# Norm's roots and their spreading taken apart, and six operands made one product earlier, in a hybrid retention block

## The chip, the core and the metric

The kernel runs on one core of one Trainium2 chip. Its engines work side by side, each through a queue of its own: TensorE (PE; its weight loads are listed as PEld), VectorE (DVE), ScalarE (ACT), GpSimd (POOL, nearly unused here) and SyncE (SP), which issues most of the transfers. The metric is the device time of one execution in microseconds, as the median of several runs.

## What is computed

One layer on 1024 tokens of 1024 channels, in float32: `h = x + 0.5 SwiGLU_1(RMSNorm(x))`, then a mixing layer, then a second SwiGLU, then a last RMSNorm. Cut to what the change touches:

```python
h = h + 0.5 * swiglu_ffn(rmsnorm(h, norm_ffn1), ffn1_w_in, ffn1_w_out)
u = rmsnorm(h, norm_mix)
proj = u @ w_in                     # q, k, v, gates and pooled part
```

Here `rmsnorm(x, g) = x * rsqrt(mean(x*x) + eps) * g`, the mean being over the channels of a token, and `swiglu_ffn(x) = (silu(x @ gate) * (x @ up)) @ w_out`. The change lies where the first SwiGLU's last product ends and the projection of the mixing layer begins.

## The kernel before

**Precision.** Each float32 operand is split in two: a high half by ScalarE (lines 157 to 163, a cast) and the rest, the low half, by VectorE. A product takes three matmuls, high by high, high by low and low by high (`mm3`, lines 176 to 180). So each operand of 128 x 512 costs one cast on ScalarE and one operation on VectorE, and each weight tile the same. `operand` (line 165) makes such a pair in a buffer of the tag mv (28 of them); `weights` (line 170) makes one in a buffer of the tag wt (5).

**Seven products.** The large products are done in Strassen's manner, on blocks of half the size. In the groups of the projection (`strassen`, named t0, t1, p0, ... after what they project) the seven products are L11 by R11, S2 by T2, S1 by T1, S3 by T3 (body `b7`, line 492, which asks for the bank `e`), L12 by R21 (`b2`, line 499, which adds to the bank `a` of the first), S4 by R22 and L22 by T4 (`b4`). L and S are blocks of the weights and their combinations, R and T blocks of the normalised input and theirs. The first two groups, t0 and t1, are taken together, product by product, in this order.

**The input of the projection.** The object `mix` of the class `Next` gathers it: the rows of the first SwiGLU's result, multiplied by the channel gains, are split into R11, R22, R21, T1 to T4. The division by the root of each token is not done on the operands but on the results of the products (`mix.rms()`, a tile of 128 x 1024 named n2rb). For it, squares are added up in the tile n2ssq as results appear (`square`, line 255). `stats` (line 398) then does two things. `roots` adds over the channels with small matmuls (`token_sums`, line 224, into the bank n2sum, line 228) and takes the inverse root of 8 numbers per partition (`inverse_root`, line 206: lines 214 to 221, a root on ScalarE and five small operations on VectorE). `rows` spreads the result over the partitions, in two halves (`spread`, line 232). For each half, the numbers are split in two in the single buffer r2, ScalarE (line 245) and VectorE (line 243) each scale four 128 x 128 identity squares by them, and two matmuls with a matrix of ones add these up in a bank (n20b and n21b, line 246), which ScalarE copies out (line 406).

**The first SwiGLU's second half** is `ffn_out` (line 813). It makes its seven products P1, P6, P2, P7, P5, P3 and P4, each in 11 steps over the inner dimension. A step has a `prep`, which loads and splits weights and operand, and a `body` with its 12 matmuls. P3 multiplies by blocks R22 and P4 by blocks T4, both read from DRAM by `both` (line 840), which loads two steps' blocks into one buffer of the tag tl (4 of them). The names in the trace are bp3w and bp3m, bp4w and bp4m for weights and operands of these products, and bp6b for P4's four banks. After P4's last step, `after4` (line 987) adds the last rows and calls `end(4)`.

**What sets the order.** `Flow.run` (line 65) calls each step's `prep` four steps ahead of its `body`, and after each `body` takes two pieces of work from a queue, `flow.back`. `end_of` (line 1095) fills that queue at the end of P2, P5, P3 and P4; after P4 it adds R21 and T4 (four pieces each, lines 331 and 337), and then `roots` and `rows`. So the program has R21, T4, roots and spread between the bodies of the first products of t0 and t1, and the spread just ahead of S3 by T3 of t0. This program order is a preference: when the program is built, each engine's queue is filled by Tile with what is ready first, the earlier in the program having precedence. Buffers and banks of one tag go round.

Of the kernel before, what the change touches and what calls it, by code (L numbers as in the profile page):

```python
# [21 lines left out]
H = S // 2  # L22
DFF = 2816
FT = DFF // P
FH = FT // 2
# [65 lines left out]
def block_kernel(ctx: ExitStack, tc, x, x_tok, vecs, f1_in, f1_out, w_in, w_v, pool_w, w_ret, w_pool, w_o,  # L91
# [16 lines left out]
    def mv(name):  # L108
        return sb.tile([P, 2, H], F32R, tag="mv", bufs=N_MV, name=name)
# [26 lines left out]
    def load(dst, src):  # L136
        nc.sync.dma_start(dst, src)
# [8 lines left out]
    def half(t, j):  # L146
        return t[:, j * H : (j + 1) * H]
# [9 lines left out]
    def split(hi, lo, src):  # L157
        copy(hi, src)  # L158
        tt(lo, src, hi.bitcast(F32), SUB)  # L159
# [5 lines left out]
    def operand(src, name):  # L165
        m = mv(name)
        split(m[:, 0], m[:, 1], src)
        return m

    def weights(src, name, at=0):  # L170
        w = wt(name, at)
        n = src.shape[-1] // P
        split(flat(w, 0, n), flat(w, 1, n), src)
        return w

    def mm3(dst, w, m, start, stop):

        mm(dst, w[0], m[0], start=start, stop=False, skip_group_check=True)  # L178
        mm(dst, w[0], m[1], start=False, stop=False, skip_group_check=True)  # L179
        mm(dst, w[1], m[0], start=False, stop=stop, skip_group_check=True)  # L180

    def parts(m, at=slice(None)):
        return m[:, 0, at], m[:, 1, at]
# [629 lines left out]
    def ffn_out(nx, ops, ready, w, res, name, sink, end, last=None):  # L813
# [3 lines left out]
        R, T, B, T4 = ops  # L817
# [22 lines left out]
        def both(key, k, src):  # L840

            if k % 2 == 0:
                t[key] = (tl if key[0] != "L" else raw)(f"{name}{key}{k}")
                n = min(2, FH - k)
                for z in range(n):
                    load(half(t[key], z), src(k + z))
            return half(t[key], k % 2)
# [53 lines left out]
        def p3(k):  # L901
            return half(S2[k // 2], k % 2), both("R22", k, lambda z: T[z][:, H:])

        def p4(k):
            return both("L22", k, lambda z: w[z, :, 2 * H : 3 * H]), both("T4", k, lambda z: T4[z])

        bk = {}

        def step(n, f, k, where, start, after):
            o = {}  # L910

            def prep():
                L, X = f(k)
                o["w"] = weights(L, f"{name}{n}w{k}")
                o["m"] = operand(X, f"{name}{n}m{k}")

            def body():
                if start and k == 0:
                    for i in range(4):
                        bk[where, i] = (sum_bank if where == "b" and i < N_SUM else bank)(f"{name}{n}{where}{i}")  # L920
                for i in range(4):
                    mm3(bk[where, i], parts(o["w"], i), parts(o["m"]), start and k == 0, k == FH - 1)
                    if k == FH - 1:
                        after(i)

            return prep, body
# [75 lines left out]
        if not last:  # L1002
            for k in range(FH):
                yield step("p4", p4, k, "b", False, after4)
            return

        L, X = {}, {}
# [4 lines left out]
        def near(k):  # L1012
            def prep():
                l, r = p4(k)
                scale(r, r, 0)
                L[k], X[k] = operand(l, f"{name}p4w{k}"), mv(f"{name}p4m{k}")
                split(X[k][:, 0], X[k][:, 1], r)

            def body():
                if k == 1:  # L1020

                    last.seed(2, bk["a", 0])
                    last.seed(3, bk["a", 1])
                for n in range(2):
                    turned(n, k)
                    if k == FH - 1:
                        last.finish(n)

            return prep, body
# [56 lines left out]
    def ffn1():  # L1086
        for n, step in enumerate(ffn_in(first, f1_in, ops1, "a", lead)):
            flow.rate = 1
            yield step
        flow.rate = 2  # L1090
        yield from ffn_out(first, ops1, ops_done["a"], f1_out, x, "b", mix.quarter, end1)
# [2 lines left out]

    def end_of(nx):
        def end(part):
            nx.work(*{2: (nx.r11,), 5: (nx.r22, nx.p22), 3: (nx.t2, nx.t1, nx.t3), 4: (nx.r21, nx.t4_)}[part])
            if part == 4:
                nx.stats()

        return end

# [529 lines left out]
    def after(nx):  # L1632

        def t2(i):
            nx.r22(i)
            nx.t2(i)

        return {0: nx.r11, 4: nx.r21, 1: t2, 3: nx.t3, 2: nx.t1, 6: nx.t4_, 5: nx.p22}
# [179 lines left out]
    def second():  # L1818
        for n, step in enumerate(ffn_in(ffn2, f2_in, ops2, "c")):
            flow.rate = 1  # L1820
            yield step
        flow.rate = 2
    flow.run(chain(ffn1(), projections(), retention(), merge(), second(),
                   ffn_out(ffn2, ops2, ops_done.setdefault("c", set()), f2_out, h2, "d", fin.quarter, fin.end, fin)))
    flow.some(-1)

# [85 lines left out]
```

## Time and profile before

| | us |
|---|---|
| median of 3 runs | 2161.24 |
| lowest and highest | 2161.03, 2163.37 |
| profiled execution | 2160.41 |
| its span, first to last instruction | 2158.6 |
| mean granted TensorE clock | 0.998 |

The profile is of one execution. Times in it count from the start of the span. A row of the timeline has the start, the time from it to the end of the last instruction of the group, the engine, the line, the operation, what is written and read, the count, and in brackets the idle time of the engine ahead of it with what ended it. Durations of neighbouring instructions overlap by some hundredths on VectorE and ScalarE, and by nearly half on TensorE.

In that execution P3 runs from 573.5 to 603.4, P4 from 603.5 to 633.4, and the first products of t0 and t1 follow.

### The profile page before, as it was taken

The numbers are of one execution on the slowest core, as the hardware profiler recorded it, in microseconds if no ns is written. First come the engines' busy times: TensorE is split into PE (matmuls) and PEld (weight loads), VectorE is DVE, ScalarE is ACT, GpSimd is POOL, SyncE is SP. The second block draws the span as 40 slices with busy tenths as digits, with TensorE's granted clock in tenths as the row PEclk, the third lists the DMA queues.
The fourth block names the chain that finished last, engine by engine and source line by source line (L and its number), as shares of the span: only waits on it lengthen the run. The fifth ranks groups of instructions, "written<-read, shape, count | busy, mean of one in ns | idle before, by whom it ended". The sixth has DMA issues, their size and how long they took to land.

```text
span 2158.6 us, 29681 instructions
## 1 busy us (share of the span) xinstructions
PE 2143.2 (99%) x10668; PEld 1813.2 (84%) x10668; DVE 1849.4 (86%) x3247; ACT 1089.6 (50%) x2049; POOL 0.2 (0%) x4
## 2 busy tenths in 40 slices
PE   9999999999999999999999999999999999999998
PEld 7888888888887888888888898887888888888887
DVE  8788888997988798899767877899988878899796
ACT  8544454453655444444426754446644544445454
POOL 0000000000000000000000000000000000000000
PEclk9999999999999999999999999999999999999999
DMA  7232423585522333333485567624123232358642
GB/s 256 84 123 74 138 83 127 181 290 178 183 95 102 114 127 108 107 118 109 156 273 185 167 222 256 229 93 161 69 89 132 74 128 92 127 180 290 198 131 99
DMA packets 120131, 320.91 MB, mean 149 GB/s; under 512 B 13232, under 2 KB 17456, under 8 KB 119984
## 3 DMA queue, kind: packets, MB, share of 16 engines
q1 hardware_dynamic: 119408, 317.98, 43.4%
q8 instruction: 83, 1.36, 0.3%
q10 hardware_dynamic: 576, 1.05, 0.1%
q14 instruction: 64, 0.52, 0.1%
HBM read 228.27 MB, written 90.70 MB: 148 GB/s over the span
## 4 chain that ended last, share of the span: by engine, by line
PE 92%; DVE 5%; ACT 1%; issue 1%; DMA 1%; SPq 0%; ACTq 0%; DVEq 0%
PE c_b L178 2%; PE c_b L180 2%; PE c_b L179 2%; PE a_b L178 2%; PE a_b L179 2%; PE a_b L180 2%; PE c_e L178 2%; PE a_e L179 2%; PE c_e L179 2%; PE a_e L178 2%; PE c_e L180 2%; PE a_e L180 2%; PE a_a L179 1%; PE a_a L180 1%; PE a_a L178 1%; PE c_a L179 1%
## 5 line engine op out<-in xcount | busy, mean ns | idle before, releaser
L179 PE MATMUL c_b<-n3T,c_wS 128*128 128x512 f32 x176 | 68.5, 389 | 0.0
L180 PE MATMUL c_b<-n3T,c_wS 128*128 128x512 f32 x176 | 68.5, 389 | 0.0
L178 PE MATMUL c_b<-n3T,c_wS 128*128 128x512 f32 x176 | 68.2, 389 | 0.0
L178 PE MATMUL a_b<-n1T,a_wS 128*128 128x512 f32 x168 | 65.4, 389 | 0.0
L179 PE MATMUL a_b<-n1T,a_wS 128*128 128x512 f32 x168 | 65.4, 389 | 0.0
L180 PE MATMUL a_b<-n1T,a_wS 128*128 128x512 f32 x168 | 65.3, 389 | 0.0
L178 PE MATMUL a_a<-n1R,a_wL 128*128 128x512 f32 x120 | 46.7, 389 | 0.0
L180 PE MATMUL a_a<-n1R,a_wL 128*128 128x512 f32 x120 | 46.7, 389 | 0.0
L179 PE MATMUL a_a<-n1R,a_wL 128*128 128x512 f32 x120 | 46.7, 389 | 0.0
L179 PE MATMUL c_a<-n3R,c_wL 128*128 128x512 f32 x112 | 43.7, 390 | 0.0
L180 PE MATMUL c_a<-n3R,c_wL 128*128 128x512 f32 x112 | 43.6, 389 | 0.0
L178 PE MATMUL c_a<-n3R,c_wL 128*128 128x512 f32 x112 | 43.6, 389 | 0.0
L180 PEld LDWEIGHTS c_b<-n3T,c_wS 128*128 128x128 f32 x176 | 33.0, 188 | 6.9
L178 PEld LDWEIGHTS c_b<-n3T,c_wS 128*128 128x128 f32 x176 | 33.0, 188 | 6.9
L179 PEld LDWEIGHTS c_b<-n3T,c_wS 128*128 128x128 f32 x176 | 33.0, 188 | 6.8
L159 DVE TENSOR_TENSOR a_wS<-a_S,a_wS 128x512 fp32r<-128x512 f32 x45 | 30.6, 682 | 9.2 <-ACT a_wS L158 9.1
L178 PEld LDWEIGHTS a_b<-n1T,a_wS 128*128 128x128 f32 x168 | 31.5, 188 | 6.6
L180 PEld LDWEIGHTS a_b<-n1T,a_wS 128*128 128x128 f32 x168 | 31.5, 188 | 6.6
L179 PEld LDWEIGHTS a_b<-n1T,a_wS 128*128 128x128 f32 x168 | 31.5, 188 | 6.5
L159 DVE TENSOR_TENSOR c_wS<-c_S,c_wS 128x512 fp32r<-128x512 f32 x46 | 31.3, 681 | 3.7 <-ACT c_wS L158 3.7
L178 PE MATMUL c_e<-n3T,c_wS 128*128 128x512 f32 x88 | 34.4, 391 | 0.0
L179 PE MATMUL c_e<-n3T,c_wL 128*128 128x512 f32 x88 | 34.4, 391 | 0.0
(3067 smaller groups left out, 8053.8 us busy)
## 6 DMA issues: line engine op xcount, KB each, us to landing
c_ra<-in_f_in SPq DMA_DIRECT2D x22, 512.0 KB, 3.6
c_rb<-in_f_in SPq DMA_DIRECT2D x22, 512.0 KB, 4.3
a_ra<-in_f_in SPq DMA_DIRECT2D x21, 512.0 KB, 3.5
a_rb<-in_f_in SPq DMA_DIRECT2D x21, 512.0 KB, 4.2
t<-au SPq DMA_DIRECT2D x11, 512.0 KB, 4.2
b<-ag SPq DMA_DIRECT2D x11, 512.0 KB, 3.6
r<-au SPq DMA_DIRECT2D x11, 512.0 KB, 3.7
br<-r SPq DMA_DIRECT2D x11, 512.0 KB, 5.5
```

Of the source, the lines that this page charges most:

```text
L159: tt(lo, src, hi.bitcast(F32), SUB)
L178: mm(dst, w[0], m[0], start=start, stop=False, skip_group_check=True)
L179: mm(dst, w[0], m[1], start=False, stop=False, skip_group_check=True)
L180: mm(dst, w[1], m[0], start=False, stop=stop, skip_group_check=True)
```

## The change

Two edits. In `end_of`, the end of P4 no longer queues R21 and T4 ahead of `stats`; it hands them to `stats` as the work between its two parts, so that the queue holds `roots`, R21 and T4 (eight pieces), `rows`. In `ffn_out`, the preps of P3's steps 5 to 10 also load T4's blocks 0 to 5 and make their operands; P4's first six preps take these over. The second SwiGLU, which passes `last`, is left as it was.

```diff
+        def t4s(k):
+            return both("T4", k, lambda z: T4[z])
+
+        ahead = {}
+
         def p4(k):
-            return both("L22", k, lambda z: w[z, :, 2 * H : 3 * H]), both("T4", k, lambda z: T4[z])
+            return both("L22", k, lambda z: w[z, :, 2 * H : 3 * H]), ahead.pop(k) if k in ahead else t4s(k)
...
                 L, X = f(k)
                 o["w"] = weights(L, f"{name}{n}w{k}")
-                o["m"] = operand(X, f"{name}{n}m{k}")
+                o["m"] = X if len(X.shape) == 3 else operand(X, f"{name}{n}m{k}")
+                if n == "p3" and not last and k >= FH // 2:
+                    z = k - FH // 2
+                    ahead[z] = operand(t4s(z), f"{name}p4m{z}")
...
     def end_of(nx):
         def end(part):
-            nx.work(*{2: (nx.r11,), 5: (nx.r22, nx.p22), 3: (nx.t2, nx.t1, nx.t3), 4: (nx.r21, nx.t4_)}[part])
             if part == 4:
-                nx.stats()
+                nx.stats(between=[lambda f=f, i=i: f(i) for f in (nx.r21, nx.t4_) for i in range(4)])
+            else:
+                nx.work(*{2: (nx.r11,), 5: (nx.r22, nx.p22), 3: (nx.t2, nx.t1, nx.t3)}[part])
```

## The prediction

> **What bounds the kernel now.** I read the page first, then TensorE's waits, then the windows around the longest of them, then the timeline there. The page says that TensorE is the bound. The waits show how little of it is idle, and that the two longest waits are at line 246, the two matmuls that spread the roots of mix.
>
> ```profile
> PE 2143.2 (99%) x10668; PEld 1813.2 (84%) x10668; DVE 1849.4 (86%) x3247; ACT 1089.6 (50%) x2049; POOL 0.2 (0%) x4
> PE n20b L246 <- ACT n20dg L245: 2.3, 1, 2.3
> PE n21b L246 <- ACT n21dg L245: 1.6, 1, 1.6
> PE t0b L178 <- ACT t0v L479: 0.9, 1, 0.9
> ```
>
> The windows show a second cost behind the waits. The columns are the stretch, its length, then busy time with the count for PE, PEld, DVE, ACT and POOL, the granted clock, the DMA share and GB/s. The clock is at half from 662 to beyond 668, and only there.
>
> ```profile
> 650.00:655.00 5.00, 5.00 (x31) 4.34 (x30) 5.00 (x9) 3.29 (x6) 0.00 (x0) 1.00 0.01 3
> 655.00:660.00 5.00, 3.57 (x16) 2.63 (x14) 4.93 (x14) 4.52 (x9) 0.00 (x0) 1.00 0.27 88
> 662.00:664.00 2.00, 0.55 (x1) 0.50 (x2) 0.71 (x4) 1.40 (x5) 0.00 (x0) 0.50 0.55 203
> 666.00:668.00 2.00, 2.00 (x6) 1.52 (x6) 0.00 (x0) 0.00 (x0) 0.00 (x0) 0.50 0.00 0
> ```
>
> The timeline of TensorE gives the loss. A matmul in the undisturbed stream starts 0.227 us after the one before it (its duration of 0.39 overlaps the next).
>
> ```profile
> 658.18 0.39 PE L180 MATMUL t1a<-n2R,t1wL 128*128 128x512 f32 x1
> 660.86 1.02 PE L246 MATMUL n20b<-n20dg,ones_r 128*128 128x512 f32 x2 [2.29 <-ACT n20dg L245]
> 663.45 1.22 PE L246 MATMUL n21b<-n21dg,ones_r 128*128 128x512 f32 x2 [1.57 <-ACT n21dg L245]
> 664.47 0.63 PE L178 MATMUL t0e<-n2T,t0wS 128*128 128x512 f32 x1
> 668.74 0.41 PE L179 MATMUL t0e<-n2T,t0wS 128*128 128x512 f32 x1
> ```
>
> The last product of L12 and R21 lets the next matmul in at 658.41. The next product, S3 by T3 (t0e), starts at 664.47, and its first ten matmuls take 4.27 us where the full pace takes 2.27. So it stands as if it had begun at 666.47 at full pace. From 658.41 that is 8.06 us, of which four spreading matmuls need 0.9. **About 7.15 us are lost here**, and that is nearly all there is to win at this place.
>
> Why does TensorE stand still? VectorE has no free moment before the spread. After the last sum of squares it works on without a gap; the sums on TensorE were ready long before VectorE took them up.
>
> ```profile
> 645.40 0.68 DVE L265 TENSOR_TENSOR n2ssq<-n2ssq,n2q 128x512 f32<-128x512 f32 x1
> 646.00 1.40 DVE L163 SCALAR_TENSOR_TENSOR n2R<-bacc,vec,n2R 128x512 fp32r<-128x512 f32 x2
> 647.33 0.68 DVE L159 TENSOR_TENSOR t0wS<-t0rb,t0wS 128x512 fp32r<-128x512 f32 x1
> 647.93 1.41 DVE L163 SCALAR_TENSOR_TENSOR n2R<-bacc,vec,n2R 128x512 fp32r<-128x512 f32 x2
> 651.12 1.84 PE L228 MATMUL n2sum<-cst,n2ssq 128*128 128x1 f32 x16
> 655.51 1.28 DVE L159 TENSOR_TENSOR n2T<-bacc,n2T 128x512 fp32r<-128x512 f32 x2
> 656.72 0.15 DVE L214 TENSOR_SCALAR n2v<-n2sum 128x8 f32<-128x8 f32 x1
> 656.80 0.68 DVE L454 TENSOR_TENSOR t0S<-t0ra,t0S 128x512 f32<-128x512 f32 x1
> 658.00 0.19 DVE L216 RECIPROCAL n2r<-n2r 128x8 f32<-128x8 f32 x1
> 658.22 0.17 DVE L218 TENSOR_TENSOR n2t<-n2r,n2v 128x8 f32<-128x8 f32 x1
> 658.42 0.17 DVE L219 SCALAR_TENSOR_TENSOR n2t<-n2t,n2r 128x8 f32<-128x8 f32 x1
> 659.11 0.16 DVE L221 SCALAR_TENSOR_TENSOR n2r<-n2t,n2r 128x8 f32<-128x8 f32 x1
> 659.86 0.68 DVE L159 TENSOR_TENSOR t0wL<-t0rb,t0wL 128x512 fp32r<-128x512 f32 x1
> 660.47 0.86 DVE L243 TENSOR_SCALAR n20dg<-cst,n20r 128x128 fp32r<-128x128 f32 x4
> ```
>
> Note one more thing: t0e had its weights from 648.0 on (t0wS, third row), and still stands behind both spreads. Its bank is asked for behind theirs in the program, and the banks of one tag seem to be handed out in that order. So L12 by R21, whose banks are open, is all that can cover the spread, before and after.
>
> **The change, part by part.** *The roots move.* In the program they now follow the four last additions, ahead of R21 and T4; the spread follows T4 as before. The sums need n2ssq, complete at 646.08. TensorE is then in the product S1 by T1, and the 16 small matmuls fall into it: the same 1.84 us, only earlier, so TensorE reaches L12 by R21 at 652.8 as now. I take 0 for it; 0.6 us is the upper end, if TensorE's queue holds the sums ahead of that product, which began at 645.52. VectorE gets n2v at about 648.6, behind three of the R21 operations. Its five small operations cost 0.15 + 0.19 + 0.17 + 0.17 + 0.16 = 0.84 us, and the root is there at about 650.5, nine microseconds earlier than at 659.27.
>
> *What that delays.* The 0.84 us are not new, but they now lie ahead of T4 and of the weights of L12. The low half of those weights is what L12 by R21 waits for:
>
> ```profile
> 652.99 0.68 DVE L159 TENSOR_TENSOR t0wL<-t0ra,t0wL 128x512 fp32r<-128x512 f32 x1
> 653.85 0.40 PE L180 MATMUL t0a<-n2R,t0wL 128*128 128x512 f32 x1
> ```
>
> Four matmuls with the high half run from 652.8 to 653.7, and then TensorE waits. With 0.84 us more on VectorE, and some rounding of its order, the wait grows by **0.9 us** (ends: 0, if the order puts these weights first; 1.5, if a combination of weights slips in as well).
>
> *What that brings.* T4's last operation (the row at 655.51) now ends 0.9 later, at about 657.6, and the spread follows at once. The root's wait is gone, and so is the work that ran ahead of the spread: from 656.80 to 660.47 VectorE made two combinations S4 and three low halves of weights. These five, 3.0 us, stand behind the spread in the program and can follow it, since their products come after t0e and t1e. ScalarE scales its four squares earlier, in its own gaps. VectorE's four take 0.86, so the first half of the spread is complete at about 658.6. The second half uses the one buffer r2 again, so it cannot start earlier; from the end of VectorE's first four (661.33) to n21b (663.45) it took 2.12 us. So n21b starts at 660.7, and t0e 0.5 us after it, at **661.25**.
>
> *What TensorE does until then.* L12 by R21 ends at 658.41 + 0.9 = 659.3, and the two matmuls of n20b, taken in between, make it 659.8. It waits **0.9 us** for n21b. So the gain is 666.47 - 661.25 = **5.2 us**, which is the 7.15 lost now less two waits of about 0.9 each and rounding.
>
> *The clock.* That sum leaves out the half clock. In the trace the pause of 0.9 at t0b (645.5) left it at full, and 2.29 + 1.57 us with two matmuls between them halved it for some 6 us. Two pauses of 0.9, six microseconds apart, lie by the first; if the clock fell after them as it does now, the ten slow matmuls' 2.0 us would come back and make 2158.1. The Trainium skill ("TensorE: Matmul & The Clock Gate", Part 1) has the clock fall after an idle window of about 3.4 us. No single pause here is that long and the clock fell all the same, so the rule holds here at best for a mostly idle window. By the rule the sum keeps its 5.2.
>
> *What is late next.* The five deferred operations end near 663.3; S4 by R22 starts two products after t0e, at 661.25 + 5.45 = 666.7. The raw buffers that they free are reloaded later by about 2 us, against a first reader 15 us on:
>
> ```profile
> 657.54 0.33 SPq L137 DMA_DIRECT2D p0ra<-in_w_in  x1
> 672.64 0.63 ACT L158 CAST p0wL<-p0ra 128x512 fp32r<-128x512 f32 x1
> ```
>
> VectorE's idle time up to 670 takes the deferred work:
>
> ```profile
> 670.03 0.69 DVE L1132 TENSOR_TENSOR t0B<-t0b,t0p 128x512 f32<-128x512 f32 x1 [7.32 <-ACT t0p L496]
> ```
>
> *Six operands in P3.* The trace shows that they are there already. The first row below is the timeline's, the next two are groups of VectorE and ScalarE within P3 (573.5 to 602), with exactly six of them; two windows follow:
>
> ```profile
> 586.43 1.29 DVE L159 TENSOR_TENSOR bp3m<-bR,bp3m 128x512 fp32r<-128x512 f32 x2
> L159 DVE TENSOR_TENSOR bp4m<-bT,bp4m 128x512 fp32r<-128x512 f32 x6 | 3.9, 684 | 0.0
> L158 ACT CAST bp4m<-bT 128x512 fp32r<-128x512 f32 x6 | 3.5, 615 | 0.7 <-DMA bT<-m 0.7
> 592.00:602.00 10.00, 10.00 (x46) 8.29 (x45) 2.99 (x5) 2.50 (x4) 0.00 (x0) 1.00 0.36 109
> 602.00:612.00 10.00, 10.00 (x46) 8.28 (x45) 10.00 (x18) 4.26 (x8) 0.00 (x0) 1.00 0.44 145
> ```
>
> They ran ahead because nothing held them, and VectorE was then 70% idle for ten microseconds before the full stretch that starts at 602. The edit puts them still earlier, with their six loads ahead of R's last on SP's queue. I take **0**. Ends: -3.6 us, if they came out of the full stretch (six VectorE operations, one every 0.6 us); and no loss up to some 7 us of delay, since P3's last operand of R is made at 587.7 and the product that uses the first of the last three starts near 595.
>
> **Sum.** The profiled execution took 2160.41 (span 2158.6, 1.8 around it). 2160.41 - 5.2 = 2155.2. The median of the runs shown is 0.83 above it, so the forecast is **2156.1**, own range 2154.8 to 2157.6.
>
> **Rivals.**
> *The cover is complete.* VectorE's scalings slip into gaps between T4's operations, and n21b is ready before L12 by R21 ends. For it: ScalarE's T4 conversions sit between VectorE's. Against it: VectorE showed no gap there. Gain 6 to 7.2: 2154.0 to 2155.2.
> *Given back.* The deferred 3.0 us still run ahead of the spread, because the order on VectorE is set at build by what is ready. Then n21b starts near 663.5, and the halved clock stays: gain 0 to 3, 2158.3 to 2161.3. For it: before, the S4 combinations slipped between the root's steps.
> *Slower.* The order of TensorE's queue puts both spreads ahead of L12 by R21's remaining 20 matmuls, for example because the build takes the scalings to be quicker. The Trainium skill (the same page, Part 2) says that matmuls stay in program order and only weight loads are pulled ahead; t0e, ready and waiting behind n21b, agrees. TensorE then stands from 653.7 to 660.7, loses some 2 us to the clock, and has 4.6 us of matmuls behind that: t0e in effect at 668.3 and 1.9 slower, 2163.1; with the spread at 663.45 as now it is 4.6 slower, 2165.8. It decides from the point at which 23 of the 24 are held back (5.2 / 0.227). Against it: TensorE takes what is ready, and in the trace it took L12 by R21 first.
> *Part two relieves P4* after all: 3.6 more, 2152.5. Against it: the six in the row above.
>
> **How the numbers follow.** Forecast 0.53, complete cover 0.13, given back 0.22, slower 0.09, part two 0.03. About 0.2% (4.3 us) is what a measurement of this kernel can tell from no change, that is 2156.9 and 2165.6. A fifth of the forecast's own range, all that is given back and half of the slower case lie between: 0.11 + 0.22 + 0.05 = 0.38. Faster: 0.42 + 0.13 + 0.03 = 0.58, of which I take 0.57; slower: 0.05. The range reaches from complete cover to given back, with the 0.6 of the sums on top: 2153.5 to 2162.0; part two and the slower case stay outside.
>
> **What would show it.** Right: the 16 small matmuls inside S1 by T1 near 646 to 648; the root at 650 to 651; no S4 combination on VectorE ahead of n20dg; n21b's wait under 1.2 us; the clock at 1.00 from 660 to 670; a wait of t0a for t0wL of about 1 us; six bp4m in P3 as before. Wrong: n21b still after 663, a row with half clock, L12 by R21 behind n21b in TensorE's order, or a new wait past 670, where nothing is forecast.

## The result, and the profile after

| | before, us | after, us |
|---|---|---|
| median | 2161.32 (2159.64 to 2164.83, 20 runs) | 2158.38 (2156.21 to 2162.04, 20 runs) |
| profiled execution | 2160.41 | 2156.45 |
| its span | 2158.6 | 2154.7 |

The ratio is 0.9986, with an interval of 0.9979 to 0.9992: faster by 2.9 us, and by the interval by 1.7 to 4.5. The forecast was 2156.1, with a gain of 5.2; 2158.4 lies outside its own range (2154.8 to 2157.6) and inside the wide one (2153.5 to 2162.0).

Two single profiles differ by more than the change. Up to the first matmul of S1 by T1 the two are already 1.08 us apart, though the edits move nothing there but six operands. So I measure the change in the stretch that it touches: from the first matmul of S1 by T1 (t0b) to the first of the product p0a. Here are its ends in TensorE's timeline of the kernel before, and the first matmul after t0e's twelve:

```profile
645.52 0.50 PE L178 MATMUL t0b<-n2T,t0wS 128*128 128x512 f32 x1 [0.94 <-ACT t0v L479]
...
669.22 0.40 PE L178 MATMUL t1e<-n2T,t1wS 128*128 128x512 f32 x1
...
682.84 0.39 PE L178 MATMUL p0a<-n2R,p0wL 128*128 128x512 f32 x1
```

and the same view of the kernel after, with what lies between:

```profile
644.44 0.50 PE L178 MATMUL t0b<-n2T,t0wS 128*128 128x512 f32 x1 [0.93 <-ACT t0v L479]
645.48 1.84 PE L228 MATMUL n2sum<-cst,n2ssq 128*128 128x1 f32 x16
652.93 0.50 PE L180 MATMUL t0a<-n2R,t0wL 128*128 128x512 f32 x1
...
653.96 0.39 PE L246 MATMUL n20b<-n20dg,ones_r 128*128 128x512 f32 x1
...
656.06 0.50 PE L180 MATMUL t1a<-n2R,t1wL 128*128 128x512 f32 x1 [0.35 <-DVE t1wL L159]
...
658.24 0.39 PE L180 MATMUL t1a<-n2R,t1wL 128*128 128x512 f32 x1
659.39 0.49 PE L246 MATMUL n20b<-n20dg,ones_r 128*128 128x512 f32 x1 [0.76 <-DVE n20dg L243]
661.46 0.74 PE L246 MATMUL n21b<-n21dg,ones_r 128*128 128x512 f32 x2 [1.58 <-ACT n21dg L245]
662.04 0.57 PE L178 MATMUL t0e<-n2T,t0wS 128*128 128x512 f32 x1
...
666.38 0.39 PE L178 MATMUL t1e<-n2T,t1wS 128*128 128x512 f32 x1
680.00 0.39 PE L178 MATMUL p0a<-n2R,p0wL 128*128 128x512 f32 x1
```

The stretch went from 37.31 to 35.56 us, **1.75 us shorter**. The rows say how (starts counted from the first row of each kernel). The last matmul of L12 by R21 starts at 12.66 before and 13.80 after: 1.14 later, of which one matmul of n20b taken in on the way is 0.23. From there to t0e it is 6.29 before and 3.80 after: 2.49 earlier. The twelve matmuls of t0e take 4.75 before (664.47 to 669.22) and 4.34 after: 0.41 less. 2.49 + 0.41 - 1.14 = 1.76.

TensorE's waits of the kernel after show that neither wait at the spread is gone:

```profile
PE n21b L246 <- ACT n21dg L245: 1.6, 1, 1.6
...
PE n20b L246 <- DVE n20dg L243: 0.8, 1, 0.8
```

The wait at n20b fell from 2.3 to 0.8; that at n21b is the same 1.6. The windows (in the columns of the prediction) show that the half clock is still there, for a shorter time:

```profile
662.00:664.00 2.00, 2.00 (x6) 1.59 (x5) 1.24 (x2) 0.92 (x2) 0.00 (x0) 0.52 0.67 240
664.00:666.00 2.00, 2.00 (x7) 1.54 (x7) 0.00 (x0) 0.00 (x0) 0.00 (x0) 0.62 0.79 231
666.00:668.00 2.00, 2.00 (x11) 1.62 (x10) 0.80 (x2) 1.10 (x2) 0.00 (x0) 1.00 0.08 31
```

VectorE's timeline of the kernel after has the reason for the late spread. Two places in it were not in the forecast: the 1.70 us in which VectorE stands still for n2sum, and the operations between T4's last multiplication (656.52) and the scalings of the second half (660.52).

```profile
644.91 0.75 DVE L163 SCALAR_TENSOR_TENSOR n2R<-bacc,vec,n2R 128x512 fp32r<-128x512 f32 x1
647.36 0.17 DVE L214 TENSOR_SCALAR n2v<-n2sum 128x8 f32<-128x8 f32 x1 [1.70 <-PE n2sum L228]
...
651.45 0.16 DVE L221 SCALAR_TENSOR_TENSOR n2r<-n2t,n2r 128x8 f32<-128x8 f32 x1
...
656.52 0.75 DVE L342 SCALAR_TENSOR_TENSOR bacc<-bacc,vec,bacc 128x512 f32<-128x512 f32 x1
657.19 0.16 DVE L159 TENSOR_TENSOR n20r<-n2r,n20r 128x4 fp32r<-128x4 f32 x1
657.26 0.69 DVE L454 TENSOR_TENSOR t0S<-t0ra,t0S 128x512 f32<-128x512 f32 x1
657.86 0.28 DVE L243 TENSOR_SCALAR n20dg<-cst,n20r 128x128 fp32r<-128x128 f32 x1
658.06 0.69 DVE L159 TENSOR_TENSOR n2T<-bacc,n2T 128x512 fp32r<-128x512 f32 x1
658.66 0.68 DVE L243 TENSOR_SCALAR n20dg<-cst,n20r 128x128 fp32r<-128x128 f32 x3
659.25 0.69 DVE L159 TENSOR_TENSOR t0wS<-t0S,t0wS 128x512 fp32r<-128x512 f32 x1
659.85 0.16 DVE L159 TENSOR_TENSOR n21r<-n2r,n21r 128x4 fp32r<-128x4 f32 x1
659.92 0.69 DVE L454 TENSOR_TENSOR t1S<-t1ra,t1S 128x512 f32<-128x512 f32 x1
660.52 0.87 DVE L243 TENSOR_SCALAR n21dg<-cst,n21r 128x128 fp32r<-128x128 f32 x4
```

The root is ready at 651.6, and the first scaling by it begins at 657.86. It is not the root that the spread waits for now, it is VectorE's queue.

**The theory**, then: the gain is limited by where the spread stands on VectorE. With T4 ahead of it, the pauses of TensorE shrink but stay, and the clock, which falls after two pauses close together, takes back what the first pause gave. The rivals: the single buffer r2 ties the halves together and that alone is the cost; the early roots cost VectorE a stall that eats their gain; or part two, the six operands, costs or gives something.

### The profile page after: what moved, and what is told of

Read it like the earlier page. It is cut to its first block, busy times and chain, and to the rows that moved or that the text cites. A ratio compares the mean times of both kernels' runs of the same rounds, so it can differ in the third digit from the quotient of the medians.

```text
span 2154.7 us, 29677 instructions
## 1 busy us (share of the span) xinstructions
PE 2140.9 (99%) x10668; PEld 1813.5 (84%) x10668; DVE 1849.2 (86%) x3247; ACT 1088.3 (51%) x2049; POOL 0.2 (0%) x4
## 4 chain that ended last, share of the span: by engine, by line
PE 95%; DVE 3%; ACT 1%; DMA 0%; issue 0%; SPq 0%; ACTq 0%; DVEq 0%
PE c_b L178 2%; PE c_b L180 2%; PE c_b L179 2%; PE a_b L178 2%; PE a_b L179 2%; PE a_b L180 2%; PE c_e L178 2%; PE c_e L179 2%; PE a_e L179 2%; PE a_e L178 2%; PE c_e L180 2%; PE a_e L180 2%; PE a_a L179 1%; PE a_a L178 1%; PE a_a L180 1%; PE c_a L179 1%
```

## The experiments

Each edit is shown against the kernel after. This table holds the measurements: the starts of S1 by T1's, n21b's, t0e's and p0a's first matmul in TensorE's timeline, the stretch between the first and the last of these, how many matmuls in it ran at half clock, and the median, with the ratio to the kernel before in the same comparison (whose medians lie at 2160.92 to 2161.32).

| | S1·T1 | n21b | t0e | p0a | stretch | half clock | median, us | ratio, interval |
|---|---|---|---|---|---|---|---|---|
| before | 645.52 | 663.45 | 664.47 | 682.84 | 37.31 | 12 | 2161.32 | |
| after | 644.44 | 661.46 | 662.04 | 680.00 | 35.56 | 8 | 2158.38 | 0.9986, 0.9979 to 0.9992 |
| e1 roots only | 645.77 | 662.78 | 663.35 | 681.33 | 35.56 | 8 | 2159.10 | 0.9993, 0.9984 to 1.0002 |
| e2 operands only | 645.04 | 663.26 | 664.28 | 682.25 | 37.21 | 11 | 2160.27 | 0.9999, 0.9990 to 1.0008 |
| e3 spread before T4 | 646.37 | 657.78 | 658.36 | 676.96 | 30.58 | 0 | 2153.14 | 0.9966, 0.9954 to 0.9979 |
| e4 R21, roots, spread, T4 | 645.70 | 659.22 | 659.73 | 676.06 | 30.36 | 0 | 2154.71 | 0.9974, 0.9965 to 0.9984 |
| e5 two buffers r2 | 646.14 | 661.66 | 662.00 | 678.59 | 32.45 | 0 | 2155.80 | 0.9974, 0.9965 to 0.9983 |
| e6 roots after two of R21 | 645.55 | 662.14 | 662.71 | 679.07 | 33.52 | 7 | 2156.79 | 0.9984, 0.9975 to 0.9993 |
| e7 products repeated | 645.82 | 662.49 | 662.71 | 679.28 | 33.46 | 0 | 2156.98 | 0.9982, 0.9973 to 0.9991 |
| e10 as e4, no operands | 645.99 | 659.45 | 660.00 | 676.34 | 30.35 | 0 | 2153.97 | 0.9971, 0.9960 to 0.9982 |
| e11 t0e's bank first | 646.00 | 665.14 | 653.40 | 676.36 | 30.36 | 0 | 2155.79 | 0.9977, 0.9967 to 0.9986 |
| e12 as e3, two r2, no operands | 645.16 | 655.52 | 655.98 | 675.36 | 30.20 | 0 | 2153.23 | 0.9967, 0.9954 to 0.9979 |

The runs of several experiments overlap; the stretch tells more, since it repeats to 0.1 us where nothing in it was changed (after and e1: 35.56 and 35.56; e4 and e10: 30.36 and 30.35). It is of one execution each, though, and what the clock did in that execution is part of it.

**The two parts apart.** e1 leaves out the operands, e2 restores the old queue.

```diff
# e1
-                o["m"] = X if len(X.shape) == 3 else operand(X, f"{name}{n}m{k}")
-                if n == "p3" and not last and k >= FH // 2:
-                    z = k - FH // 2
-                    ahead[z] = operand(t4s(z), f"{name}p4m{z}")
+                o["m"] = operand(X, f"{name}{n}m{k}")
# e2
+            nx.work(*{2: (nx.r11,), 5: (nx.r22, nx.p22), 3: (nx.t2, nx.t1, nx.t3), 4: (nx.r21, nx.t4_)}[part])
             if part == 4:
-                nx.stats(between=[lambda f=f, i=i: f(i) for f in (nx.r21, nx.t4_) for i in range(4)])
+                nx.stats()
```

> The roots' move alone; the six operands are made in P4's preps as before. I measure the stretch from the first matmul of S1 by T1 of t0 to the first matmul of p0: 37.31 us in the trace of before, 35.56 in that of after. Theory A (all of the change's gain is the roots' move; the operands were made in P3 anyway): stretch 35.6, time about 2158.4, as after. Rival B (the operands bring part of it): stretch above 36, or P4 or P3 longer than the 30.0 us that each takes now, and a time of 2159.5 or more.

> The six operands alone; R21, T4, roots and spread in the order of before. Theory A: stretch 37.3, P3 and P4 30.0 each, time within 0.05% of before. Rival B: 1 to 2 us faster than before, with P4 or what follows it shorter.

e1 has the stretch of the kernel after to the hundredth, e2 that of before within 0.1. In the traces part two is worth nothing. The medians are less sharp: e1's 2159.10 lies between the times of its two expectations, and its interval reaches 1.0002; e2 is by the medians 0.72 us below before. So some 0.7 us either way are not excluded by the times. The groups of the kernel after, from 540 to 604, show the same six as before, only earlier (the first now at 569.7):

```profile
L159 DVE TENSOR_TENSOR bp4m<-bT,bp4m 128x512 fp32r<-128x512 f32 x6 | 4.1, 685 | 0.0
```

From 592 to 602 VectorE is idle for 6.45 of 10 us (7.01 before), P3 takes 29.92 us there (30.02 before, 30.02 and 30.05 in e1 and e2), and from P4's first matmul to S1 by T1 it is 42.03 to 42.05 us in every kernel of the table.

**The spread ahead of T4.** e3 puts only R21 between the roots and the spread, e4 leaves the roots behind R21 too, so that against before T4 alone moves in the queue, behind roots and spread.

```diff
# e3
-                nx.stats(between=[lambda f=f, i=i: f(i) for f in (nx.r21, nx.t4_) for i in range(4)])
+                nx.stats(between=[lambda i=i: nx.r21(i) for i in range(4)])
+                nx.work(nx.t4_)
# e4
-                nx.stats(between=[lambda f=f, i=i: f(i) for f in (nx.r21, nx.t4_) for i in range(4)])
+                nx.work(nx.r21)
+                nx.stats()
+                nx.work(nx.t4_)
```

> The change, but with the spread queued ahead of T4: roots, R21, spread, T4. Theory V (what VectorE does ahead of the spread's scalings sets the end of the spread, and T4's eight operations are 5 us of it): n21b starts near 656 instead of 661.5, before L12 by R21 is done, which then covers what is left; the clock stays at 1.00; stretch about 30.8, time about 2153.6. Rival R (the spread is as early as the roots and the chain through ScalarE and the one buffer r2 allow, T4's place does not matter): stretch 35 to 36, time as after, 2158.4.

> The six operands of the change, but R21 first, then roots, spread, T4: the roots are late, as before, and only T4 is behind the spread. Theory V: VectorE no longer stands 1.7 us for the sums, n21b starts near 658, about when L12 by R21 ends; clock at 1.00; stretch about 30.4, time about 2153.2. Rival R (the early roots are what brings the gain): the root is taken some 1.5 us later than in after, so the stretch is above 36 and the time between after and before, 2159 to 2161.

Both cut 5 us more off the stretch (35.56 to 30.58 and 30.36). e3's time is as expected; e4's median is 1.5 above its 2153.2, and the intervals of the two overlap. In e4 the order on VectorE, and TensorE's rows behind it, are these:

```profile
654.81 0.15 DVE L221 SCALAR_TENSOR_TENSOR n2r<-n2t,n2r 128x8 f32<-128x8 f32 x1
...
656.16 0.86 DVE L243 TENSOR_SCALAR n20dg<-cst,n20r 128x128 fp32r<-128x128 f32 x4
656.95 0.74 DVE L342 SCALAR_TENSOR_TENSOR bacc<-bacc,vec,bacc 128x512 f32<-128x512 f32 x1
...
658.29 0.86 DVE L243 TENSOR_SCALAR n21dg<-cst,n21r 128x128 fp32r<-128x128 f32 x4
```

```profile
658.99 0.39 PE L180 MATMUL t1a<-n2R,t1wL 128*128 128x512 f32 x1
659.22 0.67 PE L246 MATMUL n21b<-n21dg,ones_r 128*128 128x512 f32 x2
659.73 0.39 PE L178 MATMUL t0e<-n2T,t0wS 128*128 128x512 f32 x1
```

n21b follows L12 by R21 with no wait, t0e follows n21b, and no window of the stretch is below a clock of 1.00. All of the loss at the spread is gone, and it goes without roots ahead of R21: e4 is as short as e3. e4's root is not as late as before, however, since T4 stands behind the roots too: it is there 9.26 us after S1 by T1's start (the row at 654.81), against 13.75 before and 7.17 after. Its first scalings, at 10.5, needed a root earlier than 13.75. So an earlier root is needed for this gain and does not bring it by itself. e3, which differs from the kernel after in the order of spread and T4 alone, shows what was left: T4 ahead of the spread.

**One buffer or two.**

```diff
-        r2 = sb.tile([P, 2, 8], F32R, tag="r2", bufs=1, name=f"{name}r2")
+        r2 = sb.tile([P, 2, 8], F32R, tag="r2", bufs=2, name=f"{name}r2")
```

> The change with two buffers r2 in place of one, so that the second half of the spread need not wait for the first; stretch from S1 by T1 of t0 to the first matmul of p0 (37.31 before, 35.56 after, 30.4 to 30.6 with T4 behind the spread). Theory V with r2 as the second cause: both halves' scalings run in one piece once VectorE comes to them, n21b near 660.0 instead of 661.5 (in the time of after), no pause above about 1 us, clock at 1.00; stretch about 32.3 (33.9 if the clock still falls), time about 2155. Rival (r2 does not matter, since the first half is late itself): stretch 35 to 35.6, time 2158.4.

With T4 ahead, the single buffer costs 3.1 us (35.56 to 32.45). TensorE's timeline of e5:

```profile
661.19 0.50 PE L246 MATMUL n20b<-n20dg,ones_r 128*128 128x512 f32 x1 [0.83 <-DVE n20dg L243]
661.66 0.50 PE L246 MATMUL n21b<-n21dg,ones_r 128*128 128x512 f32 x1
662.00 0.40 PE L178 MATMUL t0e<-n2T,t0wS 128*128 128x512 f32 x1
```

The second half is ready with the first; the pause of 1.58 is gone, and with one pause of 0.83 left no matmul is slow. About 1.5 us of the 3.1 are the pause and 1.6 are the eight slow matmuls, 0.2 each. The medians differ by 2.6. So the rival of the buffer names a real cost, but T4's place is worth 5.0 with the one buffer left as it is, and with the spread early the second buffer is worth 0.4 (e12, below).

**The stall for the sums.** e6 puts two pieces of R21 ahead of the roots.

```diff
-                nx.stats(between=[lambda f=f, i=i: f(i) for f in (nx.r21, nx.t4_) for i in range(4)])
+                flow.add(*(lambda i=i: nx.r21(i) for i in range(2)))
+                rest = [lambda i=i: nx.r21(i) for i in range(2, 4)]
+                nx.stats(between=rest + [lambda i=i: nx.t4_(i) for i in range(4)])
```

> The change with the roots queued behind R21's first two pieces instead of ahead of all. In after VectorE's queue held n2v so early that it stood 1.70 us for the sums on TensorE. Theory S (that stand is time lost to the spread): the stand shrinks to about 0.5 us, n21b comes about 1.2 us earlier; stretch about 34.4, or 32.8 if the pauses then leave the clock at full; time 2155.6 to 2157.2. Rival (the stand was slack, ScalarE or TensorE ends the wait): stretch 35.6, time 2158.4.

VectorE and TensorE in e6:

```profile
648.59 0.17 DVE L214 TENSOR_SCALAR n2v<-n2sum 128x8 f32<-128x8 f32 x1 [0.55 <-PE n2sum L228]
...
659.06 0.67 DVE L243 TENSOR_SCALAR n20dg<-cst,n20r 128x128 fp32r<-128x128 f32 x3
```

```profile
646.59 1.96 PE L228 MATMUL n2sum<-cst,n2ssq 128*128 128x1 f32 x16
648.41 0.77 PE L179 MATMUL t0b<-n2T,t0wS 128*128 128x512 f32 x1
...
662.14 0.73 PE L246 MATMUL n21b<-n21dg,ones_r 128*128 128x512 f32 x2 [1.56 <-ACT n21dg L245]
```

The stall falls from 1.70 to 0.55 us. VectorE's first four scalings end 14.2 us after S1 by T1's start instead of 14.9, and t0e starts at 17.16 instead of 17.60: of 1.15 us of stall, 0.44 reaches TensorE. The stretch is shorter by 2.04; the other 1.60 come from the clock, which stays at 1.00 at the spread in this execution. It is at half somewhere else: seven matmuls behind the sums, from 648.41 on, start 0.43 us apart (the last section says why there). They make L12 by R21 end later, and that filled the pause ahead of n20b. So the 2.04 are not the price of the stall, and e6 by itself does not settle it between its two expectations; its rows do.

**The clock.** e7 does more than the kernel after: it makes n20b's sum four times over, each time the same sum into the same bank, so that six matmuls more stand in the pause.

```diff
-        b = bank(f"{name}b")[:, : n * P]
+        b, both = bank(f"{name}b")[:, : n * P], []
...
+            both.append(dg)
+        if name == "n20":
+            for _ in range(3):
+                for z in range(2):
+                    mm(b, ones_r, both[z], start=not z, stop=bool(z))
```

> The change with the two matmuls of the first half of the spread done four times over into the same bank, which gives the same sum: six matmuls more, 1.4 us of TensorE, in the pause before n21b. Theory C (the pauses of 0.8 and 1.6 us are what halves the clock, which costs 1.6 us over t0e's first eight matmuls): with the pause filled no matmul is slow, and the kernel gets faster by doing more: stretch about 33.5, time about 2156.5. Rival (the clock falls for another reason, such as the sums or the little work since 655): eight slow matmuls as in after, stretch 35 to 35.6.

TensorE's timeline of e7:

```profile
660.76 0.50 PE L246 MATMUL n20b<-n20dg,ones_r 128*128 128x512 f32 x1 [0.76 <-DVE n20dg L243]
661.10 1.55 PE L251 MATMUL n20b<-n20dg,ones_r 128*128 128x512 f32 x6
662.49 0.39 PE L246 MATMUL n21b<-n21dg,ones_r 128*128 128x512 f32 x1
```

Six more matmuls make the stretch 2.1 us *shorter* (35.56 to 33.46). n21b comes 16.67 after S1 by T1 instead of 17.02, and none of t0e's matmuls is slow. The half clock is thus the work of the pauses, and its price in the profiled execution of the kernel after is eight times 0.2, about 1.6 us.

**As e4, but without the six operands.** The edit is e1's and e4's together.

> R21, roots, spread, T4 as in the run of that name, without the six operands. If these bring nothing in any order: stretch 30.4, P3 and P4 30.0 each, time as with them, about 2154.7. If they do: 1 us or more slower.

30.35 against 30.36, and P3 and P4 as long as ever: in the trace part two is worth nothing in the better order either (the medians: 0.74 us less without the operands, where after has 0.72 less with them).

**Whose bank comes first.** The prediction supposed that t0e, ready early, waits only because the spread asks for its banks first. e11 adds two empty pieces of work, so that t0's S3 by T3 asks first.

```diff
-                nx.stats(between=[lambda f=f, i=i: f(i) for f in (nx.r21, nx.t4_) for i in range(4)])
+                nx.stats(between=[lambda f=f, i=i: f(i) for f in (nx.r21, nx.t4_) for i in range(4)]
+                         + [lambda: None] * 2)
```

> The changed kernel with two empty pieces of work between T4's and the rows, so that t0's body product S3·T3 asks for its banks ahead of the spread. Theory (a product whose operands are ready waits behind the spread only because the spread asks for its banks first): S3·T3 follows S1·T1 on TensorE without a pause, L12·R21 comes after it, and the halves of the spread are covered by these products although T4 still stands ahead of them on VectorE; the stretch from S1·T1 to p0a is about 30.4 us (30.2 to 31.0), the granted clock stays at 1.00, the time is about 2153.3 us. Rival (t0's S3·T3 is held by its own operands, or the later evacuations of L12·R21 are held by the late spread and give the time back): 35 to 36 us, and about 2158 us.

TensorE's timeline of e11:

```profile
653.40 0.39 PE L178 MATMUL t0e<-n2T,t0wS 128*128 128x512 f32 x1
...
665.14 0.61 PE L246 MATMUL n21b<-n21dg,ones_r 128*128 128x512 f32 x2
...
683.36 0.50 PE L178 MATMUL p0b<-n2T,p0wS 128*128 128x512 f32 x1 [1.19 <-ACT p0wS L158]
```

t0e starts 7.40 us after S1 by T1 instead of 17.60, right behind the same product of t1; no wait is left at the spread although T4 still stands ahead of it on VectorE, and the stretch is 30.36 as the theory had it. The supposition about the banks holds, and T4's place costs what it does only where the spread's banks are asked for ahead of t0e's. The time is not the 2153.3 expected: a new wait of 1.19 us stands behind the stretch, at p0b, as the rival said, only smaller; it is 1.19 of some 2.5 us, and the rest is open. Counted from S1 by T1, p0b's weights are cast at 36.68 in e11 and at 35.00 in e3. VectorE was idle, waiting for ScalarE, for 1.77 of the 5 us from 665 to 670 (0.08 in e3). That its work then crowds what follows and makes these weights late is my reading; no run tests it.

**Both costs out, and no operands.** e12 is e3 with e5's second buffer and e1's edit.

> Roots, R21, then the spread ahead of T4 on VectorE, as in the experiment with the spread ahead of T4, with two buffers for the spread's bank, and without the six operands made during P3. If the order on VectorE was nearly all of the cost and the single buffer costs nothing once the spread comes early, the stretch is 30.3 us (30.2 to 30.6) and the time about 2153 us, as with one buffer. If the single buffer still serialises the halves, it is 0.3 us or more shorter than the 30.58 us with one buffer; if the six operands matter, it is 1 us or more longer in P4.

The stretch is 30.20, 0.38 shorter than e3's; e3's last wait, 0.23 ahead of n21b, is gone. The median is 2153.23, against 2153.14 of e3: the runs cannot tell these two apart. So the single buffer still costs a wait with the spread early, but a small one. Both kernels beat the one before by 0.33% or 0.34% (0.21% to 0.46%), and the one after too: the slowest runs of e3 and e12 (2155.25 and 2156.13) are below the fastest of after (2156.21), and the medians of before in these comparisons differ by 0.33 at most.

## Why the prediction was right or wrong

The time lay in the range, and the direction was right. The gain at the place itself was 1.75 us, not 5.2, and that is the rival "given back" (0 to 3), not the forecast. That the time lay in the range is owed to the range's width, which took in this rival; the mechanism of the forecast failed at one step.

*What bounds the kernel* was right. e3, e4 and e12 show stretches of 30.2 to 30.6, 6.7 to 7.1 shorter than before: nearly all of the 7.15 us that the prediction called lost was there to win. The reason given for t0e's waiting, the order of the banks, is shown by e11.

*What the roots delay* was right: the sums fell inside S1 by T1 at no cost, and L12 by R21 ended 1.14 later, 0.9 of it waits, 0.23 the taken-in n20b matmul that the prediction counted apart. Only, more than half of the waits was at t1a for t1wL (the row at 656.06 comes 0.74 after the one before it), and not at t0a for t0wL, as forecast.

*What that brings* is the step that failed, with two terms. The first is the stated order, "VectorE gets n2v at about 648.6, behind three of the R21 operations", and then the spread "at once" behind T4's last operation, with five operations "behind the spread". The built queue has n2v behind one operation of R21, where VectorE stands for 1.70 us with ready work behind it; the root is there 7.2 us after S1 by T1's start instead of 5.0; and t0S stands ahead of the first scalings, t0wS and t1S ahead of the second. The first half was complete 14.9 us after S1 by T1's start, and the forecast's 658.6 is 13.1: 1.8 late. t0S is 0.6 of it; by e6's 0.72 for 1.15 us of stall, the 1.70 make about 1.1, an estimate. The second half then took the forecast's 2.12 us to n21b (659.34 to 661.46). So n21b came 1.8 late, at 17.02 instead of 15.2.

The second term is *the clock*. The prediction saw that it could fall, priced it at 2.0 us and took nothing, since it forecast two pauses of 0.9 far apart. There were 0.76 and 1.58, half a microsecond apart, with one matmul between them, and eight matmuls were slow: 1.6 us. 1.8 and 1.6 are 3.4, and 5.2 less 3.4 is the 1.75 measured, to 0.05. The rule by which the sum kept its 5.2 did not hold as it was read there (last section).

*Complete cover*, rated at 0.13, is what e4 reaches, by another order. *Slower* did not occur: the matmuls of L12 by R21 were not held. What was put against it, that TensorE takes what is ready, is not what the traces show, though: before, t0e had its weights at 648.0 and stood behind n21b until 664.47. *Part two* was right at 0, in three comparisons (after with e1, before with e2, e4 with e10).

The rest, from 1.75 in the stretch to 2.94 in the medians, is inside the interval (1.7 to 4.5), and no run explains it. Part of it can be the clock: shifted along the two traces, the windows of the last section catch the pauses of before in at least nine positions of ten and those of after in a third to a half (an estimate, by the bounds found there), so an average execution of the kernel after would lose less than 1.6 at the spread. Left untried is the wait of 0.9 at t0b for ScalarE's t0v, which every kernel here has.

## What to carry to other kernels

Ask of a moved step where the in-order queue of each engine will hold it, and what ready work stands behind it there: moving the root six and a half microseconds ahead (from 13.75 to 7.17 behind S1 by T1's start) brought little, since the scalings that use it stayed behind T4 on VectorE, while moving T4 behind both root and scalings (e4) brought four times as much. Where a product with ready operands waits, look at who asks for its bank first; and where an operand or result is wanted early, give it its second buffer only after its place in the queue. Count two short pauses close together as one for the clock, price the matmuls that it slows, and expect that price in some executions and not in others.

## What the runs showed of the hardware

Pauses far shorter than the slow stretch halve the clock when they lie close together: 0.76 and 1.58 us with one matmul between them (after, and 0.76 and 1.57 in e1) made eight matmuls slow; one of 0.83 (e5), one of 1.56 with TensorE full before it (e6), one of 1.19 (e11) and the 0.9 at t0b made none by themselves.

The traces also show when the clock changes. Within one trace all changes lie whole multiples of 3.413 us apart: 661.91 and 668.74 before (two), 662.09 and 665.51 after (one), and from the first record of the clock, at 6.55 before, to 661.91 there are 192. So the stretch can be cut into these windows. Below are two of before, two of after, and one each of e6 and e7, in the columns of the prediction:

```profile
658.50:661.91 3.41, 1.07 (x3) 0.37 (x2) 3.06 (x12) 2.73 (x9) 0.00 (x0) 1.00 0.97 330
661.91:665.32 3.41, 1.87 (x4) 1.50 (x5) 0.81 (x4) 2.08 (x6) 0.00 (x0) 0.50 0.39 130
658.68:662.09 3.41, 1.12 (x4) 0.72 (x5) 2.86 (x12) 2.63 (x8) 0.00 (x0) 1.00 0.66 171
662.09:665.51 3.42, 3.42 (x10) 2.68 (x9) 1.15 (x2) 0.83 (x2) 0.00 (x0) 0.50 0.71 219
644.76:648.17 3.41, 2.62 (x19) 2.44 (x20) 3.28 (x6) 3.13 (x5) 0.00 (x0) 1.00 0.20 77
660.30:663.71 3.41, 2.95 (x13) 2.31 (x14) 3.16 (x11) 2.81 (x8) 0.00 (x0) 1.00 0.69 198
```

In all twelve traces the clock fell behind every window with matmuls busy for 1.34 us or less (1.07 before, 1.12 after, 1.34 in e1), and behind none with 1.62 or more (1.62 is e1's, from 2148.43), if the small matmuls of the sums are left out. They must be for e6: 1.58 of the 2.62 us before its fall are theirs. There the pause of 0.94 and most of the sums lie in one window; in the other kernels with early sums a boundary parts the two or cuts the sums. At half clock a full window brought full speed back (after), and one with 1.87 us did not (before). Where the windows lie differs between executions: the end of the window at the spread is 16.4 us behind S1 by T1's start before and 16.3 in e6, 17.65 in after and 17.85 in e1. In e5 and e7 it is 17.69 and 17.89, as in after and e1, so it was not the windows' place that spared these two.

The Trainium skill ("TensorE: Matmul & The Clock Gate", Part 1) speaks of an idle window of about 3.4 us that runs freely and does not start anew with the kernel, and of about as much busy time before full speed returns. The traces agree with the length, with the free running and with the way back. They differ in one thing: the window need not be idle, since one with 1.34 us of matmuls in 3.41 halved the clock. Where between 1.34 and 1.62 the limit lies, no run shows.
